# A 64-byte gap behind each pair of activation rows, and weight tiles moved to the same place mod 256 bytes

## The chip, the cores and the metric

The kernel runs on one core of a Trainium2 chip. The metric is the device time of one execution in microseconds (us); lower is better. The kernel is built as one program for five engines (TensorE, called PE in the profile, with its weight loads as PEld; VectorE, DVE; ScalarE, ACT; GpSimd, POOL; SyncE, SP), which wait for each other with semaphores.

## The reference

One layer of a hybrid decoder trunk, batch 1, 256 positions, model width 2048, all in float32:

```
hn  = rmsnorm(x, norm_mix_g)
p   = hn @ w_in + b_in                          # 2048 -> 6152 columns
u   = silu(group_norm(causal_conv31(p_a * sigmoid(p_g))))        # 1024 channels
hm  = group_norm(mlstm(silu(conv4(p_q, p_k)), p_v, gates)) * sigmoid(p_o)
x   = x + concat(u, hm) @ w_out                 # 2048 -> 2048
hf  = rmsnorm(x, norm_ffn_g)
up  = hf @ w_up                                 # 2048 -> 2 * 5632
x   = x + (silu(causal_conv3(up_gate)) * up_value) @ w_down      # 5632 -> 2048
out = rmsnorm(x, norm_final_g)
```

## The kernel before

**Split numbers.** Every large product is made from float32r parts: a number is its rounded part "hi" and the rest "lo", and hi\*hi + hi\*lo + lo\*hi is summed in PSUM. A matmul has two operands in SBUF: the weights, which a LDWEIGHTS puts into the array (128 columns, 512 bytes of each partition), and the moving operand, which streams through (256, 344 or 512 columns).

**Slabs.** The weight matrices come from HBM in slabs of two row tiles of 128 rows (`nk=2`, mostly 512 columns wide, 4096 bytes in each partition). A slab lands in `raw` (5 buffers), ScalarE rounds it into `hi` (L214), VectorE or GpSimd writes the rest into `lo` (L215); `hi` and `lo` have 4 buffers each. The Python loop over `slabs` writes out the program in order: the split of a slab some slabs ahead, the matmuls of this slab, then tasks that fall due and pieces of background work (the 31-tap convolution on VectorE).

**Activations.** `xp` holds the transposed, gained x: 16 row tiles (`kt`), of each a hi row of 256 words and a lo row of 256 words, so `[P, NK, 2, T]`, 2048 bytes for each `kt` and 4096 bytes for the two that belong to a slab. `x1p` holds the same for x1 = x + mix, in the same place. `gfb` takes the place once more at the end for the final gain. ScalarE writes the hi row (L931 for x, L645 for x1) and VectorE the lo row.

**Stages, in order of time, and which operand is which:**

- ws (`ws_group`, L241 to L243, 7 to 249 us, with O in between): columns a, g, q, k of `w_in`. Weights: 128-column pieces of `hi` or `lo`; moving: a 256-column row of `xp`. 8 groups of 8 slabs, 24 matmuls for each slab: 1536.
- O and V (`xs_slab`, L286 to L288, 105 to 155 us and 249 to 302 us): columns o (344 wide) and v (512 wide) of `w_in`. Weights: pieces of `xp`; moving: rows of `hi` and `lo`.
- w_out (the same lines, 302 to 398 us). Weights: pieces of `mixh`, `mixl`; moving: `hi`, `lo`, 512 columns.
- gate and up (`wp_group`, L267 and L268, 398 to 887 us): `w_up`. Weights: pieces of `hi` (L267) and of `lo` (L268); moving: both rows of `x1p` at once (512 columns) with `hi`, the hi row alone (256 columns) with `lo`. 22 groups of 8 slabs of 8 such pairs: 1408 pairs.
- w_down (L286 to L288, and L840 to L842 for the last 512 columns, 887 to 1127 us). Weights: pieces of `ah`, `al`; moving: `hi`, `lo`, 512 columns, 256 in the very last part.

**Where the tiles lie.** The pools give out SBUF one tile behind the other, so `xp` has `ident`, `xs`/`x1` and the constants ahead of it, and everything else behind it. Byte offsets in each partition, mod 256, as the built programs have them:

| tile | before | after |
|---|---|---|
| `xs`, `x1` | 192 | 192 |
| `xp`, `x1p`, rows of slab c (c = 0 to 7) | 192 for all c | 192 + 64 c |
| `raw`, `hi`, `lo`, all buffers | 160 | 192 |
| `mixh`, `mixl` | 192 | 224 |
| `ah`, `al` | 160 | 192 |
| `y`, `z`, `yo`, `sg` (`t2k`) | 128 | 160 |

Within a tile the rows and the 128-column pieces that matmuls read are whole multiples of 256 bytes apart, with one exception: a row of the 344-wide slabs has 1376 bytes, so their second row lies 96 bytes further on mod 256.

Of the kernel before, what the change touches and what calls it, by code (L numbers as in the profile page):

```python
# [9 lines left out]
F32 = mybir.dt.float32  # L10
F32R = mybir.dt.float32r
# [4 lines left out]
P = 128  # L16
T = 256
NT = T // P
D = 2048
NK = D // P  # L20
# [15 lines left out]
AHEAD = 3  # L36
SIG = 4
WARM = (6, 5, 10)


@with_exitstack
def hybrid_layer_kernel(
# [11 lines left out]
    cst = ctx.enter_context(tc.tile_pool(name="cst", bufs=1))  # L54
# [7 lines left out]
    def mm_bank(name):  # L62
        return ps.tile([P, 512], F32, tag="mm", name=name, bufs=4)

    def cv_bank(k, name):
        return ps.tile([P, 512], F32, tag=f"cv{k}", name=name)

    def ax_bank(name):
        return ps.tile([P, 512], F32, tag="ax", name=name, bufs=2)
# [7 lines left out]
    def v2(t):  # L77
        return t.rearrange("p (a b) -> p a b", a=2)
# [65 lines left out]
    def transpose_rows(*items):  # L144
        b = ax_bank("tr")
        o = 0
        for key, dst in items:
            r, n = rows[key]
            pe.transpose(b[:, o:o + n], r[:n, :], ident[:n, :n])
            o += n  # L150
        o = 0
        for key, dst in items:
            n = rows[key][1]
            act.copy(dst, b[:, o:o + n])
            o += n
# [11 lines left out]
    def after(delay, fn, cost=0.0):  # L167
        tasks[cur[0] + delay].append((fn, cost))
# [26 lines left out]
    def split_tiles(i):  # L195
        s = slabs[i]
        n = s["nk"] * s["w"]
        raw = raw_t.pop(i)
        hi = slab.tile([P, 2 * W], F32R, tag="hi", name=f"hi{i}", bufs=SPLIT_BUFS)
        lo = slab.tile([P, 2 * W], F32R, tag="lo", name=f"lo{i}", bufs=SPLIT_BUFS)  # L200
        s["eng"] = pool if s["pool"] and i >= 8 and i % 2 else dve
        hi_t[i] = hi[:, :n].rearrange("p (k c) -> p k c", k=s["nk"])
        lo_t[i] = lo[:, :n].rearrange("p (k c) -> p k c", k=s["nk"])
        s["lo"] = 0.0 if s["eng"] is pool else 1.1 * n + 30
        return raw, hi, lo
# [11 lines left out]
    def w_slab(wap, kt, nk, col, w, fn, on_pool):  # L217
        if col is None:
            src = wap(kt)
        else:  # L220
            src = wap[kt * P:(kt + nk) * P, col:col + w].rearrange("(k p) c -> p k c", p=P)
        slabs.append(dict(src=src, w=w, nk=nk, mm=fn, pool=on_pool))
# [54 lines left out]
    def xs_slab(wap, col, w, stat, kt, first, last, st, done, on_pool):  # L277
        def fn(hi, lo):
            if first:
                st["b"] = [cv_bank(0, "xs0"), cv_bank(1, "xs1")] if st.get("cv") else [mm_bank("xs0"), mm_bank("xs1")]  # L280
            sh, sl = stat()
            for k in range(2):
                for tt in range(NT):
                    o = st["b"][tt][:, :w]
                    ts_ = slice(tt * P, (tt + 1) * P)
                    pe.matmul(o, sh[:, kt + k, ts_], hi[:, k, :w], start=first and k == 0, stop=False)  # L286
                    pe.matmul(o, sh[:, kt + k, ts_], lo[:, k, :w], start=False, stop=False)  # L287
                    pe.matmul(o, sl[:, kt + k, ts_], hi[:, k, :w], start=False, stop=last and k == 1)  # L288
            if last:
                done(st["b"])  # L290
        w_slab(wap, kt, 2, col, w, fn, on_pool)

    def xs_group(wap, col, w, stat, nk, done, on_pool):
        st = {}
        for kt in range(0, nk, 2):
            xs_slab(wap, col, w, stat, kt, kt == 0, kt + 2 == nk, st, done, on_pool)


    xT = {}
# [318 lines left out]
    def done_out(n):  # L618
        def fn(banks):
            cs = slice(n * 512, (n + 1) * 512)  # L620
            st = {}

            def ev():
                if "h2" not in xT:
                    xT["p2"] = cst.tile([P, NK, 2, T], F32R, tag="xp", name="x1p")
                    xT["h2"], xT["l2"] = xT["p2"][:, :, 0, :], xT["p2"][:, :, 1, :]
                x1 = xres["t"]
                for tt in range(NT):
                    dve.tensor_add(x1[:, tt, cs], x1[:, tt, cs], banks[tt])

            def sq():
                for tt in range(NT):
                    act.activation(banks[tt], xres["t"][:, tt, cs], AF.Square, accum_out=ssq[:, tt, n:n + 1])

            def tr(half):
                def f():
                    b = ax_bank("x1T")
                    st[half] = b
                    for k in range(2):
                        kt = 4 * n + 2 * half + k  # L640
                        for tt in range(NT):
                            pe.transpose(b[:, k * T + tt * P:k * T + (tt + 1) * P], xres["t"][:, tt, kt * P:(kt + 1) * P], ident)
                    for k in range(2):
                        kt = 4 * n + 2 * half + k
                        act.activation(xT["h2"][:, kt, :], v2(b)[:, k, :], AF.Copy, scale=g_ffn[:, kt:kt + 1])  # L645
                    for k in range(2):
                        kt = 4 * n + 2 * half + k
                        dve.scalar_tensor_tensor(xT["l2"][:, kt, :], v2(b)[:, k, :], g_ffn[:, kt:kt + 1],
                                                 xT["h2"][:, kt, :].bitcast(F32), op0=ALU.mult, op1=ALU.subtract)
                return f  # L650
            after(1, ev, 1300)
            after(2, tr(0), 800)
            after(3, tr(1), 800)
            after(3, sq)
            if n == 3:
                after(4, rs_ffn)
        return fn

    ffn = {}
# [119 lines left out]
        dve.tensor_mul(o, o, ffn["gf"][:, c0:c0 + w])  # L779

    def load_gf():
        gfb = cst.tile([P, NK, 2, T], F32, tag="xp", name="gfb")
        ffn["gf"] = gfb.rearrange("p a h b -> p (a h b)")[:, 0:D]
        act.dma_start(ffn["gf"], bass.AP(tensor=norm_final_g.tensor, offset=norm_final_g.offset, ap=[[0, P], [1, D]]))

    def done_down(n, c0, w):
        def fn(banks):
            def ev():
                if n == 0:
                    load_gf()  # L790
                for tt in range(NT):
                    add_down(banks[tt], tt, n, c0, w)

            def gmul():
                for tt in range(NT):
                    mul_gf(tt, c0, w)
            after(1, ev)
            after(3, gmul)
            if n == 2:
                after(3, pre_sum)  # L800
        return fn
# [81 lines left out]
    for b in range(3):  # L883
        xs_group(w_in, OFF_O + OW * b, OW, get_xT, NK, done_o(b), True)
# [6 lines left out]
    for hp in range(2):  # L891
        xs_group(w_in, OFF_V + 512 * hp, W, get_xT, NK, done_v(hp), True)
# [17 lines left out]
    for n in range(3):  # L910
        xs_group(w_down, 512 * n, W, lambda: (ffn["ah"], ffn["al"]), NF, done_down(n, 512 * n, W), False)
    down_last(3, 1536, W, SPLIT_BUFS)


    xT["p"] = cst.tile([P, NK, 2, T], F32R, tag="xp", name="xp")
    xT["h"], xT["l"] = xT["p"][:, :, 0, :], xT["p"][:, :, 1, :]
    for c in range(NK // 2):
        sl = slice(c * T, (c + 1) * T)
        if c:
# [4 lines left out]
    def prep_x(c, ks=(0, 1)):  # L924
        b = ax_bank("xT")
        for k in ks:
            for tt in range(NT):
                pe.transpose(b[:, k * T + tt * P:k * T + (tt + 1) * P], big[:, tt, (2 * c + k) * P:(2 * c + k + 1) * P], ident)
        for k in ks:
            kt = 2 * c + k  # L930
            act.activation(xT["h"][:, kt, :], v2(b)[:, k, :], AF.Copy, scale=g_mix[:, kt:kt + 1])  # L931
        for k in ks:
            kt = 2 * c + k
            dve.scalar_tensor_tensor(xT["l"][:, kt, :], v2(b)[:, k, :], g_mix[:, kt:kt + 1],
                                     xT["h"][:, kt, :].bitcast(F32), op0=ALU.mult, op1=ALU.subtract)
# [13 lines left out]
    def warm_pe(n):  # L949
        b = cv_bank(0, "warm")  # L950
        for k in range(n):
            pe.transpose(b[:, 0:P], ident, ident)

    warm_pe(WARM[0])
    transpose_rows(("G", g_mix))
    warm_pe(WARM[1])
    prep_x(0, (0,))
    warm_pe(WARM[2])
    first = split_tiles(0)
# [33 lines left out]
    for i in range(len(slabs)):  # L993
# [30 lines left out]
        while bg and credit > 0:  # L1024
            name = bg[0][0].__name__
# [40 lines left out]
```

## Time and profile before

| | us |
|---|---|
| three runs | 1137.03 median (1136.78 to 1137.9) |
| the profiled execution | 1136.69 |
| its span, first to last instruction | 1135.0 |
| PE busy / PEld busy | 1122.2 / 995.0 |
| DVE / ACT / POOL busy | 746.3 / 579.2 / 131.1 |
| mean granted TensorE clock | 0.998 of full speed |

The profile's times are of one execution under the hardware profiler. Its matmul records are pipelined: a record is longer than the step from one matmul's start to the next one's, and that step is what counts when matmuls follow each other without a wait. The chain of waits, read in order of time, gives those steps.

### The profile page before, as it was taken

How to read it: one execution, taken by the hardware profiler on the slowest of the kernel's cores; microseconds unless marked ns; L12 is line 12 of the kernel's file. 1: busy time of each engine (PE TensorE's matmuls, PEld its weight loads, DVE VectorE, ACT ScalarE, POOL GpSimd, SP SyncE). 2: the span in 40 equal slices, each digit the busy share in tenths (PEclk: the TensorE clock that was granted, in tenths of full speed). 3: DMA queues.
4: the chain of work that ended last, by engine and by line, in shares of the span. 5: the costliest groups of instructions: out<-in, count | busy, mean ns of one | idle time of the engine just before them, and what ended most of it. 6: DMA issues, size and time to landing. Idle time of an engine off the chain costs nothing.

```text
span 1135.0 us, 16970 instructions
## 1 busy us (share of the span) xinstructions
PE 1122.2 (99%) x6516; PEld 995.0 (88%) x6516; DVE 746.3 (66%) x1136; ACT 579.2 (51%) x822; POOL 131.1 (12%) x100
## 2 busy tenths in 40 slices
PE   8999999999999999999999999999999999999997
PEld 8999999998888888888888888888888888888886
DVE  5498999987656457667666676576676645454543
ACT  4744576754445455545545555455455534343443
POOL 0343554543200000000000000000000000000000
PEclk9999999999999999999999999999999999999999
DMA  8864665565555666666666666666666667656662
GB/s 266 254 184 127 178 220 170 179 193 176 193 197 174 184 184 184 192 197 187 185 199 190 185 189 193 192 186 188 194 194 184 191 195 230 195 191 194 193 193 90
DMA packets 122681, 215.40 MB, mean 190 GB/s; under 512 B 7440, under 2 KB 33256, under 8 KB 122088
## 3 DMA queue, kind: packets, MB, share of 16 engines
q1 hardware_dynamic: 121048, 209.92, 61.5%
q10 hardware_dynamic: 1552, 4.39, 1.0%
q8 instruction: 51, 0.84, 0.3%
q14 instruction: 30, 0.25, 0.1%
HBM read 212.19 MB, written 2.10 MB: 189 GB/s over the span
## 4 chain that ended last, share of the span: by engine, by line
PE 95%; DVE 3%; ACT 1%; issue 1%; POOL 0%; POOLq 0%; ACTq 0%
PE gate L267 14%; PE up L267 14%; PE xs L287 9%; PE xs L286 9%; PE xs L288 9%; PE up L268 7%; PE gate L268 7%; PE ws L243 5%; PE ws L241 5%; PE ws L242 5%; PE xs L841 2%; PE xs L840 2%; PE xs L842 2%; DVE conv L376 2%; DVE lo L215 1%
## 5 line engine op out<-in xcount | busy, mean ns | idle before, releaser
L215 DVE TENSOR_TENSOR lo<-raw,hi 128x1024 fp32r<-128x1024 f32 (+2 forms) x353 | 435.0, 1233 | 326.2 <-ACT hi L214 324.8
L214 ACT CAST hi<-raw 128x1024 fp32r<-128x1024 f32 (+2 forms) x400 | 411.8, 1033 | 452.5 <-PE xs L288 153.7
L267 PE MATMUL gate<-x1p,hi 128*128 128x512 f32 x704 | 245.0, 390 | 0.0
L267 PE MATMUL up<-x1p,hi 128*128 128x512 f32 x704 | 244.5, 390 | 0.0
L268 PE MATMUL up<-x1p,lo 128*128 128x256 f32 x704 | 198.5, 282 | 0.0
L268 PE MATMUL gate<-x1p,lo 128*128 128x256 f32 x704 | 198.5, 282 | 0.0
L267 PEld LDWEIGHTS up<-x1p,hi 128*128 128x128 f32 x704 | 132.2, 188 | 27.7
L267 PEld LDWEIGHTS gate<-x1p,hi 128*128 128x128 f32 x704 | 132.2, 188 | 27.6
L241 PE MATMUL ws<-xp,hi 128*128 128x256 f32 x512 | 145.1, 283 | 1.8 <-ACT hi L214 1.8
L243 PE MATMUL ws<-xp,lo 128*128 128x256 f32 x512 | 143.3, 280 | 1.5 <-DVE lo L215 1.5
L242 PE MATMUL ws<-xp,hi 128*128 128x256 f32 x512 | 143.0, 279 | 0.0
L268 PEld LDWEIGHTS gate<-x1p,lo 128*128 128x128 f32 x704 | 133.1, 189 | 0.0
L268 PEld LDWEIGHTS up<-x1p,lo 128*128 128x128 f32 x704 | 133.1, 189 | 0.0
L215 POOL TENSOR_TENSOR lo<-raw,hi 128x1024 fp32r<-128x1024 f32 (+1 forms) x48 | 110.5, 2304 | 152.4 <-ACT hi L214 114.4
L287 PE MATMUL xs<-lo,ah 128*128 128x512 f32 x264 | 102.7, 389 | 0.0
L286 PE MATMUL xs<-hi,ah 128*128 128x512 f32 x264 | 102.7, 389 | 0.0
L288 PE MATMUL xs<-hi,al 128*128 128x512 f32 x264 | 102.7, 389 | 0.0
L241 PEld LDWEIGHTS ws<-xp,hi 128*128 128x128 f32 x512 | 96.2, 188 | 3.0 <-ACT hi L214 2.3
L243 PEld LDWEIGHTS ws<-xp,lo 128*128 128x128 f32 x512 | 96.2, 188 | 2.5 <-DVE lo L215 2.3
L376 DVE SCALAR_TENSOR_TENSOR conv<-up,cB,conv 128x256 f32<-128x256 f32 x240 | 97.5, 477 | 0.0
L242 PEld LDWEIGHTS ws<-xp,hi 128*128 128x128 f32 x512 | 96.3, 188 | 0.0
L817 POOL TENSOR_TENSOR rf<-ms,halves 128x1 f32<-128x1 f32 x2 | 1.1, 551 | 711.7 <-DVE ms L811 711.7
(188 smaller groups left out, 1308.6 us busy)
## 6 DMA issues: line engine op xcount, KB each, us to landing
raw<-in_w_up_dram SPq DMA_DIRECT2D x176, 512.0 KB, 3.9
raw<-in_w_down_dram SPq DMA_DIRECT2D x88, 512.0 KB, 4.4
raw<-in_w_in_dram SPq DMA_DIRECT2D x48, 512.0 KB, 4.0
raw<-in_w_in_dram SPq DMA_DIRECT2D x64, 256.0 KB, 4.4
raw<-in_w_out_dram SPq DMA_DIRECT2D x32, 512.0 KB, 4.3
raw<-in_w_in_dram SPq DMA_DIRECT2D x24, 344.0 KB, 3.5
x<-in_x_dram ACTq DMA_DIRECT2D x2, 1024.0 KB, 8.0
xs<-in_x_dram SPq DMA_DIRECT2D x7, 256.0 KB, 5.3
```

What stands on the lines that cost most here:

```text
L214: act.copy(hi[:, c], raw[:, c])
L215: s["eng"].tensor_sub(lo[:, c], raw[:, c], hi[:, c].bitcast(F32))
L241: pe.matmul(o, hi[:, k, cs], mh[:, kt + k, :], start=first, stop=False, skip_group_check=True)
L242: pe.matmul(o, hi[:, k, cs], ml[:, kt + k, :], start=False, stop=False, skip_group_check=True)
L243: pe.matmul(o, lo[:, k, cs], mh[:, kt + k, :], start=False, stop=last, skip_group_check=True)
L267: pe.matmul(o, hi[:, k, cs], m2, start=first, stop=last, skip_group_check=True)
L268: pe.matmul(o[:, 0:T], lo[:, k, cs], mp[:, kt + k, 0, :], start=False, stop=last, skip_group_check=True)
L286: pe.matmul(o, sh[:, kt + k, ts_], hi[:, k, :w], start=first and k == 0, stop=False)
L287: pe.matmul(o, sh[:, kt + k, ts_], lo[:, k, :w], start=False, stop=False)
L288: pe.matmul(o, sl[:, kt + k, ts_], hi[:, k, :w], start=False, stop=last and k == 1)
L376: dve.scalar_tensor_tensor(a, up[c][:, t:t + T], cB[:, 8 * t + c:8 * t + c + 1], a, op0=ALU.mult, op1=ALU.add)
L840: pe.matmul(o, sh[:, kt, ts_], hi[:, k, c:c + cw], start=kt == first, stop=False, skip_group_check=True)
```

## The change

The two activation tiles become flat tiles of `X_WORDS` = 8192 + 7\*16 + 24 = 8328 words. A small class `Rows` stands where the views stood and finds row `k` at word `k // 2 * 16 + k * 512`, so that behind each slab's two rows 16 words (64 bytes) stay empty. The 24 words at the end move everything behind the tile by 544 bytes altogether, which is 32 mod 256, and puts `hi` and `lo` at the place mod 256 at which row 0 lies. `gfb` takes the flat tile's first 2048 words as before.

The instructions are the same: on every engine each row of the program (operation, shape, tiles, waits) stands where it stood, so no order is shown here. Only addresses differ.

```diff
+GAP = 16
+X_WORDS = NK * 2 * T + (NK // 2 - 1) * GAP + 24
...
+    class Rows:
+        def __init__(self, t, part=None):
+            self.t, self.part = t, part
+
+        def __getitem__(self, key):
+            k, rest = key[1], key[2:]
+            o = k // 2 * GAP + k * 2 * T
+            v = self.t[:, o:o + 2 * T].rearrange("p (h t) -> p h t", h=2)
+            if self.part is not None:
+                rest = (self.part,) + rest
+            return v[(slice(None),) + rest]
+
+    def x_rows(name):
+        t = cst.tile([P, X_WORDS], F32R, tag="xp", name=name)
+        return tuple(Rows(t, part) for part in (None, 0, 1))
...
-                    xT["p2"] = cst.tile([P, NK, 2, T], F32R, tag="xp", name="x1p")
-                    xT["h2"], xT["l2"] = xT["p2"][:, :, 0, :], xT["p2"][:, :, 1, :]
+                    xT["p2"], xT["h2"], xT["l2"] = x_rows("x1p")
...
-        gfb = cst.tile([P, NK, 2, T], F32, tag="xp", name="gfb")
-        ffn["gf"] = gfb.rearrange("p a h b -> p (a h b)")[:, 0:D]
+        gfb = cst.tile([P, X_WORDS], F32, tag="xp", name="gfb")
+        ffn["gf"] = gfb[:, 0:D]
...
-    xT["p"] = cst.tile([P, NK, 2, T], F32R, tag="xp", name="xp")
-    xT["h"], xT["l"] = xT["p"][:, :, 0, :], xT["p"][:, :, 1, :]
+    xT["p"], xT["h"], xT["l"] = x_rows("xp")
```

The distance between a moving row and the weights that are loaded while it streams, mod 256 (moving place minus weight place):

| stage | before | after, slab c |
|---|---|---|
| ws, gate, up | 32 | 64 c |
| V | 224 (that is -32) | -64 c |
| O, first row / second row of the slab | 224 / 64 | -64 c / 96 - 64 c |
| w_out | 224 | 224 |
| w_down | 0 | 0 |

## Rows read from the trace of the kernel before

**Rows 1.** The page: engines over the span, and the last chain by engine

```profile
PE 1122.2 (99%) x6516; PEld 995.0 (88%) x6516; DVE 746.3 (66%) x1136; ACT 579.2 (51%) x822; POOL 131.1 (12%) x100
PE 95%; DVE 3%; ACT 1%; issue 1%; POOL 0%; POOLq 0%; ACTq 0%
```

**Rows 2.** Waits of PE, longest sum first: us in total, times, longest

```profile
PE ws L241 <- ACT hi L214: 1.8, 2, 1.1
PE ws L243 <- DVE lo L215: 1.5, 3, 0.7
PE warm L952 <- POOL ident masks.py:199: 1.4, 1, 1.4
PE xs L287 <- DVE lo L215: 0.4, 1, 0.4
```

**Rows 3.** Busy time by stage: PE, PEld, DVE, ACT, POOL; clock; DMA

```profile
155.00:249.00 94.00, 94.00 (x790) 92.42 (x789) 88.41 (x181) 62.72 (x89) 46.60 (x27) 1.00 0.60 191
398.00:887.00 489.00, 489.00 (x2827) 433.61 (x2826) 328.89 (x441) 258.60 (x379) 1.93 (x4) 1.00 0.65 189
887.00:1122.00 235.00, 235.00 (x1042) 194.79 (x1041) 115.73 (x109) 95.62 (x103) 0.00 (x0) 1.00 0.59 187
```

**Rows 4.** The chain, 900 to 930 us (w_down, 512 columns): first and last piece

```profile
134 pieces in order of time: start us, us, what
899.81 0.23 PE xs L286
...
929.96 0.23 PE xs L287
```

**Rows 5.** Timeline of PE, 1121.4 to 1126.8 us (w_down, 256 columns): ends

```profile
1121.33 0.28 PE L840 MATMUL xs<-hi,ah 128*128 128x256 f32 x1
...
1126.72 0.28 PE L840 MATMUL xs<-hi,ah 128*128 128x256 f32 x1
```

**Rows 6.** The chain, 600 to 630 us (up, then gate): first and last piece

```profile
175 pieces in order of time: start us, us, what
599.83 0.23 PE up L267
...
629.99 0.23 PE gate L267
```

**Rows 7.** The chain, 210 to 219 us (ws): first and last piece

```profile
78 pieces in order of time: start us, us, what
209.93 0.12 PE ws L241
...
218.91 0.12 PE ws L243
```

**Rows 8.** The chain, 362 to 391 us (w_out): first and last piece

```profile
126 pieces in order of time: start us, us, what
361.78 0.23 PE xs L287
...
390.94 0.23 PE xs L286
```

**Rows 9.** Timeline of PE, 140 to 143.9 us (O, 344 columns): ends

```profile
139.77 0.32 PE L288 MATMUL xs<-hi,xp 128*128 128x344 f32 x1
...
143.83 0.32 PE L287 MATMUL xs<-lo,xp 128*128 128x344 f32 x1
```

**Rows 10.** The chain: four float32 matmuls of 256 columns

```profile
245.37 0.86 PE S L560 x4
```

**Rows 11.** Timeline, 600 us: matmuls and weight loads by start

```profile
600.01 0.39 PE L267 MATMUL up<-x1p,hi 128*128 128x512 f32 x1
600.01 0.19 PEld L268 LDWEIGHTS up<-x1p,lo 128*128 128x128 f32 x1
600.24 0.28 PE L268 MATMUL up<-x1p,lo 128*128 128x256 f32 x1
600.24 0.19 PEld L267 LDWEIGHTS up<-x1p,hi 128*128 128x128 f32 x1
```

**Rows 12.** Groups of PE by form: count, busy us, mean ns

```profile
L267 PE MATMUL gate<-x1p,hi 128*128 128x512 f32 x704 | 245.0, 390 | 0.0
L267 PE MATMUL up<-x1p,hi 128*128 128x512 f32 x704 | 244.5, 390 | 0.0
L241 PE MATMUL ws<-xp,hi 128*128 128x256 f32 x512 | 145.1, 283 | 1.8 <-ACT hi L214 1.8
L286 PE MATMUL xs<-hi,xp 128*128 128x512 f32 x64 | 25.9, 405 | 0.0
```

## Prediction

> **What bounds the kernel now.** I read the page first: PE is busy for 99% of the span and the chain that ended last is PE for 95% of it [rows 1]. Then the waits of PE: four kinds, 5.1 us together [rows 2]. Then the stages: in all of them PE is busy throughout, at a granted clock of 1.00, the 2.4 GHz level [rows 3]. So no other engine sets the time. What is left is how long one matmul takes to make room for the next, and this change touches nothing else: the same instructions, other addresses. The useful view is therefore the chain of waits in stretches where it runs over PE alone, from which I take the step from start to start (last start minus first start, divided by the pieces less one).
>
> **The step has a part that doesn't depend on the columns.** In w_down, 512 columns: 30.15 us over 133 steps, 226.7 ns [rows 4]. The same stage at 256 columns: the timeline has 46 rows, so 5.39 us over 45 steps, 119.8 ns [rows 5]. The difference, 106.9 ns for 256 columns, is 0.4176 ns for a column, one column for each period of 2.4 GHz. Taken off, 12.9 ns stay for each matmul. I call this the fixed part and work it out in each stage:
>
> - gate and up: 30.16 us over 174 steps [rows 6], so 346.7 ns for a pair of 512 and 256 columns; less 768 columns (320.7) that is 26.0, or 13.0 for each matmul.
> - ws: 8.98 us over 77 steps [rows 7], 116.6 ns; less 106.9, 9.7.
> - w_out: 29.16 us over 125 steps [rows 8], 233.3 ns; less 213.8, 19.5.
> - O: 27 rows, 4.06 us over 26 steps [rows 9], 156.2 ns; less 143.7, 12.5.
>
> In a steady stretch there is nothing but matmuls and their weight loads, and each load starts within the same hundredth of a microsecond as the matmul ahead of its own [rows 11], so every stream runs beside a load. Four plain float32 matmuls of 256 columns take 0.86 us, 215 ns each [rows 10], which is twice the 106.9 of the columns and only about 1 ns more, and they too have a weight load each. So the fixed part isn't the price of a load as such. It appears where the stream runs at full rate beside a load, and it differs between stages that are alike but for the places of their operands: w_down and w_out run the same three lines, and their distances mod 256 (moving less weights) are 0 and 224. My reading is that the stream and the load get into each other's way in SBUF by address. It is an inference: no row shows the meeting itself.
>
> By distance the trace then gives: 0, 12.9 (twice, 512 and 256 columns); 32, 13.0 in gate and up and 9.7 in ws; 224, 19.5 in w_out; and 12.5 for O, where half of the matmuls have 224 and half 64.
>
> On this the Trainium skill, TensorE: Matmul & The Clock Gate, in "Part 2: What happens when you issue a matmul", speaks against the change having any effect: it gives PE two independent read ports and says that loading the next weights takes no read bandwidth from the running matmul. With its fixed cost of about 2.5 ns per warm matmul (Part 1) every stage would show the same small rest at any address, and the time would stay at 1136.7 us. The trace doesn't agree: it has 9.7 to 19.5 ns, and different ones for the same shape.
>
> **The change part by part.**
>
> *w_down* (distance 0 before and after) and *w_out* (224 before and after): 0. Both operands move by the same 32 bytes. If the place itself counted and not the distance, w_out could move: 384 matmuls by 6.6 ns, 2.5 us either way. I take 0 and keep that for the range.
>
> *gate and up.* 1408 pairs, two times the 704 of [rows 12]. The distance goes from 32 to 0, 64, 128, 192 in turn, a quarter of the slabs each (c and c+4 share one). At 0 the pair is 226.7 + 119.8 = 346.5 against 346.7: nothing for 352 pairs. 64, 128 and 192 have no row of their own in this stage, 1056 pairs. From below, the shortest steps that any row has, 226.7 and 116.6: 343.3, -3.4 ns, -3.6 us. From above, w_out's step and the longest 256 step, 233.3 + 119.8 = 353.1, +6.4 ns, +6.8 us. I take the fixed part of distance 0, because O, with 64 in half of its matmuls, has nearly the same (12.5): 0.
>
> *ws.* 1536 matmuls (three lines of 512, [rows 12]). Here the fixed part is the smallest, and distance 0 has a row of the same width: 119.8 against 116.6, +3.2 ns. For slabs 0 and 4, 384 matmuls, that is +1.2 us; for the other 1152 between 0 (they stay at 116.6) and +3.7 us. By the same choice as above I take 119.8 for all: +4.9 us. Nothing covers it: PE waits 3.3 us for the split of slabs in the whole of ws [rows 2], and in the second half of ws PE is busy in 94.0 of 94 us [rows 3].
>
> *V.* 192 matmuls (three lines of 64), 224 before, now 0, 192, 128, 64. From w_out's 233.3 (same width, same places) to 226.7: -6.6 ns, -1.3 us; from below in size, slabs 0 and 4 alone, -0.3 us.
>
> *O.* 288 matmuls at 12.5, now at about 12.9: +0.1 us.
>
> *The rest.* ScalarE and VectorE write the rows in the same shapes at other addresses, and PE waits for neither in the long stages; if each of these writes took a tenth longer, it would be covered, because the chain in those stretches runs over PE alone [rows 4, 6, 7, 8]. Loads land 32 bytes further on, with five buffers ahead of PE and no wait of PE for them: 0.
>
> Sum: 4.9 - 1.3 + 0.1 = +3.7 us on the profiled execution's 1136.69 us, of which its span is 1135.0: 1140.4 us. The median of the runs, 1137.03, lies 0.34 above the profiled time; I split that and say **1140.5 us**, 0.3% over the median. A measurement of this kernel can tell about 0.2%, 2.3 us, from no change.
>
> **The rivals.**
>
> *A. No measurable change.* Either addresses don't count and the stages differ for another reason (then 1137.0), or the three unseen distances are as cheap for 256 columns as 32 is, and only slabs 0 and 4 of ws pay: 1.2 - 1.3 = -0.1 us, also 1137. For it: ws and gate, at one distance, differ by 3.3 ns, so something besides the distance counts. Against the first form: w_out and w_down. Chance 0.30.
>
> *B. Faster: at some of the distances stream and load miss each other.* The float32 row shows that the fixed part can be as low as about 1 ns. If it fell to ws's 9.7 for all matmuls at 64, 128 and 192: gate and up 1056 pairs by 6.6 ns, -7.0 us; ws +1.2; V 48 by 6.6 and 144 by 9.8 ns, -1.7 us: 1129.2 us. If it fell to 1 at just one distance: gate and up 352 by 24, -8.4 us; ws 384 by 8.7, -3.3, with +3.7 for the other three quarters; V 48 by 18.5 and 144 by 6.6, -1.8: 1126.9. It decides from where the pairs' mean saves more than (4.9 - 1.3 + 2.3) / 1408, 4 ns of 346.7, if ws pays in full. VectorE caps the gain in ws only: it is busy 88.4 of 94 us there [rows 3]. Against it: none of the seen distances is that low at full rate. Chance 0.27.
>
> *C. Slower by more: 192 is like its neighbour 224.* A load that leads the stream by 32 bytes costs 19.5; if one that leads by 64 bytes does so too, gate and up pay 352 by 13.2, +4.6 us, and ws 384 by 6.6, +2.5 us, on top of my sum (in V 48 matmuls then gain nothing back, +0.3): 1147.9 us. Chance 0.10.
>
> **How the numbers follow.** My forecast has 0.33: all four distances cost what 0 does. It is the likeliest single case, but most of its 3.7 us rests on ws, which I have from one row of another stage. Slower by over 0.2%: 0.33 + 0.10 = 0.43. Within: 0.30. Faster: 0.27. The range takes in C's 1147.9 at its upper end and B's first form at its lower end, 1129 to 1148; B's second form and worse mixtures of C stay outside, some 0.15. Within the forecast's own case the bounds of w_out (2.5 either way) give 1138 to 1143.
>
> **What would show it.** In the chain of the changed kernel, the pair in gate and up, slab by slab: the four distances repeat every four slabs (2.77 us each), so each has its own step; I expect 346.7 in all of them. In ws, 119.8 in place of 116.6. In V, 226.7 in place of 233.3. In w_out and w_down, 233.3 and 226.7 as before. A step of gate and up that is the same in all slabs while V doesn't move either would say that addresses don't count; steps that differ from slab to slab with period four would say that they do, and which distance is the good one. I am wrong if gate and up move at all by more than 2 ns a pair.

## The result, and the profile after

The changed kernel takes 1144.6 us (median; 1144.44 to 1144.82) against 1137.05 for the kernel before: ratio 1.0066, 95% interval 1.0051 to 1.0081. It is slower by 7.6 us, where 3.5 us were forecast; the time lies in the range.

The page after and its chain by engine read like [rows 1]: PE is busy for 99% of a longer span, and nothing else has taken over. Lines of the program have moved down by two (L267 is now L269, L286 is L288).

```profile
PE 1130.2 (99%) x6516; PEld 995.6 (87%) x6516; DVE 742.8 (65%) x1136; ACT 579.6 (51%) x822; POOL 131.8 (12%) x100
PE 96%; DVE 1%; ACT 1%; issue 1%; POOL 0%; POOLq 0%; ACTq 0%
```

Busy time in the stages after, with the boundaries of gate, up and w_down moved by 8 us (columns as in [rows 3]: PE, PEld, DVE, ACT, POOL, granted clock, DMA):

```profile
155.00:249.00 94.00, 94.00 (x785) 92.60 (x784) 84.72 (x177) 63.28 (x89) 44.26 (x26) 1.00 0.61 189
398.00:895.00 497.00, 497.00 (x2829) 433.72 (x2828) 328.99 (x441) 258.90 (x379) 1.93 (x4) 1.00 0.65 187
895.00:1130.00 235.00, 235.00 (x1042) 194.72 (x1041) 115.89 (x108) 95.63 (x103) 0.00 (x0) 1.00 0.60 187
```

Gate and up begin at 398 us as before, but about as many matmuls (2829 against 2827 in [rows 3]) need 497 us in place of 489. The w_down stage runs the same 1042 matmuls in the same 235 us. So the whole loss arises in gate and up. The clock is at 1.00 in all three, the 2.4 GHz level.

The chain after in the stretch of [rows 6] (start, us, what; 170 steps, 85 pairs):

```profile
171 pieces in order of time: start us, us, what
599.90 0.23 PE gate L269
...
629.84 0.23 PE gate L269
```

29.94 us for 85 pairs are 352.2 ns a pair, against 346.7. The same view of w_down, and of w_out, after:

```profile
133 pieces in order of time: start us, us, what
899.86 0.23 PE xs L290
...
929.78 0.23 PE xs L290
```

```profile
117 pieces in order of time: start us, us, what
361.91 0.23 PE xs L289
...
388.98 0.23 PE xs L288
```

29.92 us over 132 steps are 226.7 ns, 27.07 over 116 are 233.4: both as in [rows 4, 8], although both operands lie 32 bytes further on.

The starts of the matmuls in the trace, put in order slab by slab, say more than the mean (mean steps in ns; the row of before is one value for all slabs):

| distance | slabs | 512 | 256 | pair | ws |
|---|---|---|---|---|---|
| 32 (before) | all | 228.4 | 118.3 | 346.7 | 117.0 |
| 0 | 0, 4 | 234.7 | 117.1 | 351.8 | 119.5 |
| 64 | 1, 5 | 233.3 | 119.8 | 353.1 | 117.4 |
| 128 | 2, 6 | 230.7 | 120.0 | 350.7 | 118.7 |
| 192 | 3, 7 | 234.0 | 118.8 | 352.8 | 116.5 |

The four pairs are 5.4 ns above 346.7 in the mean, and 1408 by 5.4 is 7.6 us: all of the loss. Slabs 0 and 4 agree (within 0.1 ns a pair, 0.8 ns in ws), and so do 1 and 5, 2 and 6, 3 and 7, so 256 bytes more make no difference. The ws steps rise by 1.0 ns in the mean, 1.6 us over 1536, but the last matmul of ws starts only 0.5 us later than before (249.7 against 249.2 us).

### The profile page after: what moved, and what is told of

It is laid out like the page before. It is cut to its first block, busy times and chain, and to the rows that moved or that the text cites. A ratio compares the mean times of both kernels' runs of the same rounds, so it can differ in the third digit from the quotient of the medians.

```text
span 1142.7 us, 16970 instructions
## 1 busy us (share of the span) xinstructions
PE 1130.2 (99%) x6516; PEld 995.6 (87%) x6516; DVE 742.8 (65%) x1136; ACT 579.6 (51%) x822; POOL 131.8 (12%) x100
## 4 chain that ended last, share of the span: by engine, by line
PE 96%; DVE 1%; ACT 1%; issue 1%; POOL 0%; POOLq 0%; ACTq 0%
PE gate L269 14%; PE up L269 14%; PE xs L289 10%; PE xs L290 10%; PE xs L288 10%; PE up L270 7%; PE gate L270 7%; PE ws L245 5%; PE ws L243 5%; PE ws L244 5%; PE xs L859 2%; PE xs L858 2%; PE xs L860 2%; DVE conv L395 1%; DVE lo L217 0%
## 5 line engine op out<-in xcount | busy, mean ns | idle before, releaser
L269 PE MATMUL gate<-x1p,hi 128*128 128x512 f32 x704 | 248.7, 396 | 0.0
L269 PE MATMUL up<-x1p,hi 128*128 128x512 f32 x704 | 248.3, 395 | 0.0
L269 PEld LDWEIGHTS up<-x1p,hi 128*128 128x128 f32 x704 | 132.3, 188 | 31.6
L269 PEld LDWEIGHTS gate<-x1p,hi 128*128 128x128 f32 x704 | 132.3, 188 | 31.5
L288 PE MATMUL xs<-hi,ah 128*128 128x512 f32 x264 | 102.7, 389 | 0.0
```

Of the source, the lines that this page charges most:

```text
L269: pe.matmul(o, hi[:, k, cs], m2, start=first, stop=last, skip_group_check=True)
```

## The experiments

All are edits of the changed kernel. `GAP` is the gap behind a slab's two rows in words, `BASE` the word at which row 0 begins in its tile. Times are medians, ratios go against the kernel before on the same chip. Steps by slab are means from the starts of the matmuls in the trace; line numbers shift by a few from kernel to kernel. The code is cut to the lines that matter.

The theories: by **distance**, the step of a matmul depends on where its moving row lies mod 256 relative to the weights loaded beside it; by **place**, weights at a multiple of 64 bytes cost more; by **gap**, it costs that rows lie at other places from slab to slab.

**Gap without the move of the weights (gap_only).**

```diff
-X_WORDS = NK * 2 * T + (NK // 2 - 1) * GAP + 24
+BASE = 0
+X_WORDS = BASE + NK * 2 * T + (NK // 2 - 1) * GAP + 16
...
-            o = k // 2 * GAP + k * 2 * T
+            o = BASE + k // 2 * GAP + k * 2 * T
```

The change of `o` is the same in every edit that has a `BASE`, and isn't shown again.

> The gap of 64 bytes behind each slab's rows is kept, but the tail is 16 words, so hi and lo stay at 160 mod 256 as in the kernel before. Distances (rows less weights) in ws, gate and up are 32, 96, 160, 224 for slabs c = 0 to 3 and again for 4 to 7. Distance theory (the step depends on the distance mod 256 and on the order of widths in the stage): the pair of slabs 0 and 4 is 346.7 ns as before; 96, 160, 224 have their own values; if only the distance mod 64 counts, all are 346.7, ws stays at 117 and the time is 1137 us. Place theory (weights at a multiple of 64 bytes are the expensive thing): all slabs at 346.7, 1137 us. Gap theory (rows that lie at other places from slab to slab cost by themselves): pairs over 350 ns in all slabs, 1142 us or more.

1142.72 us, ratio 1.0052 (1.0035 to 1.0069). Pairs by slab: 347.2 at 32; 354.5 at 96; 347.0 at 160; 351.4 at 224. It isn't the distance mod 64 that counts, nor the weights' place. The gap theory needed all slabs over 350, and two of the four distances are not.

**The move of the weights without the gap (place_only).**

```diff
-GAP = 16
-X_WORDS = NK * 2 * T + (NK // 2 - 1) * GAP + 24
+GAP = 0
+BASE = 0
+X_WORDS = BASE + NK * 2 * T + (NK // 2 - 1) * GAP + 8
```

> No gap; everything behind the activation tile moves by 32 bytes, so that all rows and all weights lie at 192 mod 256, distance 0 in all slabs of ws, gate and up. Distance theory: every slab is like slabs 0 and 4 of the changed kernel: pairs 351.8 to 353.3 ns (+5.1 to +6.6 by 1408 pairs, 7 to 9 us), ws 119.5 to 120 (+2.5 to 3 by 1536, 4 to 5 us), V 229.3 (-0.7 us): 1147 to 1150 us, slower than the changed kernel. Place theory: pairs about 352 in all slabs, 1144 to 1145. Gap theory: 346.7, 1137.

1139.24 us, ratio 1.0021 (1.0011 to 1.003). Pair 346.7 (231.7 + 115.0) in all slabs, ws 119.9, V about 228. All three theories missed part of it: by distance 351.8 or more was expected, by place 352, and by gap ws should not have moved. At the same distance of 0 the pair takes 346.7 here and 351.8 in the changed kernel.

**A gap of 32 bytes (step32).**

```diff
-GAP = 16
-X_WORDS = NK * 2 * T + (NK // 2 - 1) * GAP + 24
+GAP = 8
+BASE = 0
+X_WORDS = BASE + NK * 2 * T + (NK // 2 - 1) * GAP + 16
```

> Gap of 32 bytes in place of 64, weights at 192 mod 256, so slab c has the distance 32 c: eight distances in one run. Distance theory: slabs 0, 2, 4, 6 have the pairs of the changed kernel's slabs 0 to 3 (351.8, 353.1, 350.7, 352.8 ns), slab 1 (distance 32) has 346.7, and slabs 3, 5, 7 (96, 160, 224) have their own; if only the distance mod 64 counts, 346.7 as well, so a mean of 349.4 and about 1141 us. Place theory: about 352 in all slabs, 1144 to 1145. Gap theory: no slab at 346.7.

1142.64 us, ratio 1.0051 (1.0036 to 1.0066). Slab 1 (32): 347.8, and 346.7 from its second pair on. Slab 5 (160): 347.9. The others 350 to 354, slab 0 (distance 0) 353.6. Distance 32 is good among other distances as well; place is refuted here, since the weights lie at 192 throughout. But a slab's distance doesn't fix its mean alone: slab 2 (64) takes 350.6 here, because its first three pairs, behind the slab at 32, run at 343 to 347; the changed kernel's slab 1, also at 64, takes 353.1.

**Rows and weights both moved by 32 bytes (both_moved).**

```diff
-GAP = 16
-X_WORDS = NK * 2 * T + (NK // 2 - 1) * GAP + 24
+GAP = 0
+BASE = 8
+X_WORDS = BASE + NK * 2 * T + (NK // 2 - 1) * GAP + 0
```

> The rows begin 8 words into their tile and everything behind moves by the same 32 bytes: rows at 224, weights at 192 mod 256, distance 32 in all slabs as in the kernel before, at other places. Distance theory: pair 346.7 ns, ws 117, V and w_out 233, 1137 us. Place theory (weights at a multiple of 64 bytes): pair about 352, 1144 us. Gap theory: 346.7, 1137.

1136.87 us, ratio 0.9999 (0.999 to 1.0009). The chain in gate and up:

```profile
173 pieces in order of time: start us, us, what
599.97 0.23 PE up L270
...
629.78 0.23 PE gate L270
```

29.81 us for 86 pairs, 346.6 ns. Other places at the same distance take the same time: with one distance throughout, the distance counts, and the place doesn't.

**Four kernels with one distance each (flat0, flat64, flat128, flat192).** Every tile lies where it lies in the changed kernel; only the rows within `xp` and `x1p` are shifted, all by the same words.

```diff
-GAP = 16
-X_WORDS = NK * 2 * T + (NK // 2 - 1) * GAP + 24
+GAP = 0
+BASE = 0
+X_WORDS = BASE + NK * 2 * T + (NK // 2 - 1) * GAP + 136
```

This is flat0. In flat64, flat128 and flat192 `BASE` is 16, 32 and 48 and the last term is smaller by as much, so that `X_WORDS` is 8328 in all four.

> The changed kernel with the gap taken out and the same words added at the tile's end: every tile lies where it lies in the changed kernel, and slab 0's rows too; only the rows of slabs 1 to 7 move, so that all have the distance 0. History theory (the step depends on the distance and on the rhythm that the matmuls before have left, so a row at another distance just ahead changes it): pair 346.7 ns in all slabs as with the place alone, ws 119.9, 1139.2 us. Larger-address theory (the distance counts mod 512 or more, which the kernel with the place alone had different): 353.3 in all slabs as in the steady part of the changed kernel's slab 0, about 1149 us.

> As the kernel with all slabs at distance 0, but the rows begin 16 words into the tile: distance 64 in all slabs, all other tiles as in the changed kernel. If each slab's own distance decides: pair 353.3 ns (steady part of slab 1 of the changed kernel), ws 117.4, V 229.5: +9.3 +0.5 -0.7 us, about 1146. History theory: the pair is another one, 340 to 350 ns, and the time 1133 to 1141.

> The same with the rows 32 words into the tile, distance 128 in all slabs. If each slab's own distance decides: pair 351.1 ns, ws 118.8, V 232.5: +6.2 +2.6 -0.1 us, about 1145.5. History theory: another pair, 340 to 350, with ws at 118.8 a time of 1135 to 1144.

> The same with the rows 48 words into the tile, distance 192 in all slabs. If each slab's own distance decides: pair 353.4 ns, ws 115.5 to 116, V 233.5: +9.4 -2.0 us, about 1144. History theory: another pair, 340 to 350, time 1126 to 1140. If both held in part, the mean of the four flat kernels says what the changing of distances from slab to slab costs: the changed kernel has the same four distances in equal parts and takes 1144.6.

1139.26 us (ratio 1.0022, 1.0013 to 1.0031), 1146.48 (1.0085, 1.0068 to 1.0102), 1144.41 (1.0067, 1.0052 to 1.0082) and 1141.84 (1.0041, 1.0026 to 1.0056). The four runs of flat192 spread from 1140.45 to 1142.11 us, and the profile is of the fastest. The chain of each in gate and up, in the same order:

```profile
175 pieces in order of time: start us, us, what
599.94 0.23 PE gate L270
...
630.11 0.23 PE gate L270
```

```profile
171 pieces in order of time: start us, us, what
599.90 0.12 PE gate L271
...
629.93 0.12 PE gate L271
```

```profile
172 pieces in order of time: start us, us, what
599.98 0.12 PE gate L271
...
629.95 0.23 PE gate L270
```

```profile
171 pieces in order of time: start us, us, what
599.79 0.23 PE up L270
...
629.82 0.24 PE gate L270
```

At 0: 30.17 us for 87 pairs, 346.8 ns. At 64: 30.03 for 85, 353.3. At 128: 29.97 us less the first 0.12, for 85, 351.2. At 192: 30.03 for 85, 353.3. So 64, 128 and 192 have a step of their own, without any change from slab to slab, and it is the step that they reach in the changed kernel. The history theory falls for these three. Distance 0 is left: 346.8 here, with slab 0's rows and all weights at the very addresses of the changed kernel, so the theory of larger addresses falls too. ws: 119.9, 117.8, 118.6 and 113.7; the last ended ws 5.1 us earlier than before (244.1 us). The mean of the four kernels is 1143.0 us. The changed kernel, with the same four distances in equal parts, takes 1144.6: the changing from slab to slab costs some 1.6 us on top.

**One slab at another distance (kick).** In `x1p` alone, the last slab's rows lie 192 bytes further on.

```diff
+X_WORDS = 8328
...
-            o = k // 2 * GAP + k * 2 * T
+            o = self.base + k * 2 * T + (self.gap if k >= NK - 2 else 0)
...
-                    xT["p2"], xT["h2"], xT["l2"] = x_rows("x1p")
+                    xT["p2"], xT["h2"], xT["l2"] = x_rows("x1p", 0, 48)
```

> The kernel with all slabs at distance 0, but in x1p alone the last slab's two rows lie 192 bytes further on: gate and up see the distance 0 in slabs 0 to 6 and 192 in slab 7. Two rhythms: the 353.3 ns of the changed kernel's slabs 0 and 4 comes from what the slab ahead (distance 192) leaves, and it lasts; then slabs 0 to 6 take 353.3 here too, +6.6 ns by 1232 pairs, +8.1 us, and slab 7 353.4, +1.2 us: about 1148.5 us against the 1139.3 of all slabs at 0. Rival (a disturbed start dies away within a slab): slabs 1 to 6 are at 346.7 again, slab 7 at 353.4, 1140.5 to 1141.5 us.

1147.97 us, ratio 1.0098 (1.0082 to 1.0113), 8.7 us over flat0. The chain in gate and up:

```profile
171 pieces in order of time: start us, us, what
599.97 0.12 PE gate L269
...
629.98 0.12 PE gate L269
```

30.01 us for 85 pairs, 353.1 ns. Slabs 0 to 6 lie at distance 0 as in flat0, and all seven take 351.8 to 353.8. The slower rhythm doesn't die away: it lasts for the 56 pairs until slab 7 comes round. At distance 0 there are two steady rhythms, and what ran ahead decides which one it is. Neither repeats one step: in flat0 pairs of about 343.5 and 350.2 ns alternate, in kick three pairs of about 349, 350 and 361 follow each other. The changed kernel's slabs 0 and 4 show the same threes.

**Steps of 16 bytes (sweep16).**

```diff
+X_WORDS = 8320
...
+                    xT["p2"], xT["h2"], xT["l2"] = x_rows("x1p", 56, 4)   # base, gap
...
+    xT["p"], xT["h"], xT["l"] = x_rows("xp", 24, 4)
```

> Distances in steps of 16 bytes, all other tiles at their places mod 256 of the kernel before: gate and up see 16 c (0 to 112 for slabs 0 to 7), ws 128 + 16 c (128 to 240). If 32-byte lines decide, 16 is like 0 or 32 and 48 like 32 or 64. If the distance counts more finely, 16, 48, 80, 112 have steps of their own. Known: gate 0, 32, 64, 96: 346.7 or 353.3, 346.7, 353.3, 354; ws 128, 160, 192, 224: 118.6, 118.6, 113.7, 118.2. No forecast of the time, which mixes them: 1138 to 1146 us.

1142.94 us (one run). Pairs in gate and up: 16: 348.6; 48: 349.9; 80: 350.2; 112: 353.0. ws: 144: 118.3; 176: 119.2; 208: 119.2; 240: 117.3; slab 4, at 192, again 114.3. These are means over whole slabs, with what the slab ahead has left in them: over its last four pairs the slab at 16 is at 346.7, like 32, the one at 112 at 353.4, like 64 and 192, and only 48 (350.9) and 80 (350.1) keep a value of their own. In this mix none is better than the best ones known.

**A good distance for each stage (mixed_best).** ws at 192, gate and up at 32, w_out at 0.

```diff
+X_WORDS = 8256
...
+                    xT["p2"], xT["h2"], xT["l2"] = x_rows("x1p", 0, 0)    # base, gap
...
+    xT["p"], xT["h"], xT["l"] = x_rows("xp", 40, 0)
...
-    bb = mid.tile([P, 2056], F32, tag="bb", name="bb")
+    bb = mid.tile([P, 2056 + 56], F32, tag="bb", name="bb")[:, 0:2056]
```

> Each stage gets the best distance seen so far, by offsets alone: xp begins 160 bytes into its tile (ws at 192), x1p at its start (gate and up at 32), hi and lo at 160 as before, and mixh, mixl move to 160 (w_out at 0). Distance theory: ws 113.7 in place of 117.0, -5.1 us; V about 229.7 in place of 233.0, -0.6; O +0.3; w_out 226.7 in place of 233.2, -2.5; gate and up 346.7: -7.9 us, about 1129 us. Rival: w_out and w_down differ for another reason than the distance (w_out stays at 233.2): 1131.4.

1130.02 us, ratio 0.9941 (0.9928 to 0.9953): faster than both kernels, 6.8 us under the one before and 14.6 under the changed one, with the same instructions. The chain in two stretches of ws, then in w_out:

```profile
81 pieces in order of time: start us, us, what
224.92 0.11 PE ws L244
...
233.99 0.11 PE ws L243
```

```profile
77 pieces in order of time: start us, us, what
59.99 0.12 PE ws L242
...
68.94 0.12 PE ws L243
```

```profile
49 pieces in order of time: start us, us, what
362.99 0.23 PE xs L289
...
373.87 0.23 PE xs L289
```

113.4 ns for ws in the first stretch, from 225 us on, and 226.7 for w_out in place of 233.3, which refutes the rival: w_out and w_down differed by their distance. The 1.1 us short of the forecast lie in ws, where the mean is 114.9. The second stretch, from 60 us on, shows why: 8.95 us over 76 steps, 117.8 ns, at the same distance and the same addresses. So ws has two rhythms as well. From 50.9 to 102.2 us 18 slabs in a row, 432 matmuls, run at 117.8 and the rest at 113.7 in the mean; by 4.1 ns that is 1.8 us. Both changes fall on a short pause at the start of a slab (a step of 201 and of 202 ns); other pauses of this length changed nothing. Whether the slower runs of flat192 had such a stretch no trace shows.

**Two places for hi and lo (two_places).** hi, `mixh`, `ah` at 0 mod 256; lo, `mixl`, `al` and the rows of `xp`, `x1p` at 192. The kernel is mixed_best with six places changed. Two are shown; the others (`X_WORDS`, `bb`, `mixh`, the start of `xp`) set the remaining tiles.

```diff
+        if i == 0:
+            slab.tile([P, 48], F32R, tag="pad", name="pad")
         lo = slab.tile([P, 2 * W], F32R, tag="lo", name=f"lo{i}", bufs=SPLIT_BUFS)
...
+        ffn["ah"] = fp.tile([P, 16 + NF * T + 48], F32R, tag="ah", name="ah")[:, 16:16 + NF * T].rearrange("p (k t) -> p k t", k=NF)
```

> hi and lo get places of their own: hi, mixh, ah at 0 mod 256; lo, mixl, al and the rows of xp and x1p at 192. In gate and up the 512-column stream (beside it lo is loaded) then has the distance 0 and the 256-column stream (beside it hi is loaded) has 192; in w_out and w_down all stay at 0; in ws two of three matmuls have 192 and one 0; V has 64 and 0. Theory of own distances (each matmul pays for its own distance): pair 226.7 + 113.7 = 340.4 ns in place of 346.7, -8.8 us; ws 115.8 against 114.9, +1.3: about 1122.5 us against the 1130.0 of the kernel with a good distance for each stage. Theory of the rhythm (the pair as a whole falls into one of a few rhythms, 346.7 or 351 to 354 were seen): pair 346.7 or more, 1131 us or more, up to 1141.

1148.82 us, ratio 1.0108 (1.0091 to 1.0125), the slowest median of all, though kick's interval overlaps. Pair 350.0 (232.1 + 117.9), ws 117.9, w_out again 233.3. The chain in w_down:

```profile
130 pieces in order of time: start us, us, what
899.89 0.24 PE xs L289
...
929.99 0.23 PE xs L289
```

30.10 us over 129 steps, 233.3 ns in place of 226.7, although in w_down every stream has the distance 0 from the load beside it. What is new there is that successive streams, and successive loads, start at other places (0, 192, 0). So the theory of own distances falls: the distance to the load beside a stream doesn't give the step by itself. One rival is left untested: the distance of a stream to the weights that it uses itself. In all other kernels this is the same as the distance to the load beside it; here in w_down it is 0, 192 and 64 in turn. The theory of the rhythm foresaw the pair, but not w_down, so its time missed as well.

## Why the prediction was right or wrong

- **What bounds the kernel, and that only PE's steps can move: right.** No other engine took over, and the clock stayed.
- **w_out and w_down unchanged: right**, 233.4 and 226.7 ns, and both_moved shows the reason: as long as all matmuls of a stage have one distance, it counts and the place doesn't.
- **Distance 0 from w_down's row: right for a kernel in which all slabs have it.** place_only and flat0 have 346.7 in gate and up, 119.9 in ws, about 228 in V: 1139.2 us, where my terms give 1140.4. That the pair fits is luck, though: the terms were 226.7 for 512 columns and 119.8 for 256, and measured were 231.7 and 115.0. A fixed part for each matmul, added up, isn't how the pair works.
- **Gate and up at 0 us: wrong, and it is the step that failed.** By the prediction's own sign (over 2 ns a pair) it was wrong here: the pair rose by 5.4. "I take the fixed part of distance 0, because O, with 64 in half of its matmuls, has nearly the same (12.5): 0." The flat kernels measured 353.3, 351.2 and 353.3 ns at 64, 128 and 192. O's row couldn't be carried over: with 344 columns, and two distances in turn, O hardly tells distances apart at all (156 to 158 ns in every kernel). The measured +5.5 ns by 1056 pairs, 5.8 us, lies within my upper bound of 6.8, which w_out's row had given; the bound was the better estimate, and not a safe one: 353.1 against the 353.3 of flat64 and flat192. The other 1.8 us are the 352 pairs at distance 0, which I had at nothing with a row behind it: they fall into the slower rhythm behind a slab at 192, as kick shows.
- **ws at +4.9 us: right in sign, too large.** At 0 the step is 119.5, near the 119.8 taken; at 64, 128 and 192 it is 117.4, 118.7 and 116.5: by steps +1.6 us, and the stage ends 0.5 us later. The 116.6 that I started from wasn't the whole stage either: in the kernel before, the mean of ws is 117.0, with a stretch at 117.8 from 52 to 103 us.
- **V at -1.3 us: too large.** The trace's mean is 231.3 ns after 233.0, -0.3 us. Only distance 0 comes near 226.7 (228.0 in flat0); with V at 64, 128 and 192 (flat192, flat128, flat64) it is 229.9, 232.4 and 233.4.
- So that the forecast came out on the right side is luck, because two errors have opposite signs: the term that carried it was overdrawn by 3 us, and the largest stage was left at 0 where it paid 7.6.
- **The rivals.** A fell in both forms. B didn't happen in gate and up, but for 256 columns alone there is a good distance: 113.7 ns at 192. C foresaw rightly that 192 is dear for the pair (353.3), but at half its price, 6.6 ns in place of 13.2; 64 is just as dear, and in ws 192 is the best of all. The Trainium skill, TensorE: Matmul & The Clock Gate, in "Part 2: What happens when you issue a matmul", says that loading the next weights takes no read bandwidth from the running matmul. One time at any address, which the prediction drew from it, is not what these runs show: with the same instructions, addresses alone took the kernel from 1130.0 to 1148.8 us. Whether the ports themselves meet, no run shows.

What stays open is the mechanism. That the stream and the weight load meet in SBUF is still only an inference: no run took a load away from beside a stream. Which pattern of places gives which rhythm was measured for the patterns above and can't yet be foretold.

## What to carry to other kernels

When PE is busy throughout, compare the steps from start to start between stages of the same shape: a difference of a few ns with no wait behind it can come from where the two operands lie relative to each other mod 256 bytes, and a pad can change it for all matmuls of a stage. Such a step belongs to a stage's whole pattern (widths, order, distances), so a row of another stage is no estimate, and not even a safe bound: the pair at 96 took 354.5 ns in gap_only, where my bound was 353.1. Measure one constant distance at a time, in the stage itself, and read more than one stretch of it. Varying the places from slab to slab or between hi and lo didn't pay here: the changed kernel lies 1.6 us above the mean of its four distances, and a good distance can be spoilt by what ran ahead of it (kick).

## What the runs showed of the hardware that wasn't expected

- At one and the same set of distances a long stretch of matmuls can run steadily at 346.7 or at 353.1 ns a pair (flat0, kick), and it doesn't return by itself within 56 pairs. ws did the same at 113.4 and 117.8 ns a matmul, the slower one for 432 matmuls (mixed_best).
- Four of the steady means lie near whole multiples of 16 periods of 2.4 GHz: 226.7, 233.3, 346.7 and 353.3 ns are 544, 560, 832 and 848 periods. Others don't, such as 351.2 ns (flat128, 843) and 117.8 ns (mixed_best, 283), so no rule follows.
- 256-column float32r matmuls ran at 113.7 to 119.9 ns, as means of ws, by where the rows lie alone (flat192, flat0).
